# The up projection's high-part products joined to 512 columns, over two sets of banks, with the work beside the projections held to its place

## The chip, the cores and the metric

The kernel runs on one core of one Trainium2 chip. The metric is device microseconds (us) of the whole kernel, one launch; lower is better. Engines: PE is TensorE (matrix products), DVE is VectorE, ACT is ScalarE, POOL is GpSimd, SP is SyncE, which issues the weight loads. PSUM is the memory into which PE accumulates, in banks of 128 x 512 fp32; SBUF is the on-chip working memory.

## The reference

One layer of a diffusion backbone for 256 latent tokens with 256 context tokens, model width 2048, all in float32:

```
qa, ka, va, qb, kb, vb, rb, gf, gb, gate_a, gate_b = proj(modulate(x, g_mix, mod_x[0], mod_x[1]))
qa, ka = apply_rope(qa, cos, sin), apply_rope(ka, cos, sin)
...                                    # the same projection of ctx
o_attn = windowed_attention(qa, ka, va, cka, cva, attn_sink)
o_gla  = latent_gla(qb, kb, vb, gf, gb, sf, sb)
x = x + mod_x[2] * merge_branches(o_attn, o_gla, rb, gate_a, gate_b, gla_norm, w_attn_o, w_gla_o, w_out)
x = x + mod_x[5] * conv_ffn(modulate(x, g_ffn, mod_x[3], mod_x[4]), w_up, conv_w, conv_b, w_down)

def conv_ffn(h, w_up, conv_w, conv_b, w_down):
    u = h @ w_up                                           # 2048 x 11264
    u = sum(up[:, j:j + T] * conv_w[j] for j in range(3)) + conv_b   # centred, along the tokens
    a, g = jnp.split(u, 2, axis=-1)
    return (jax.nn.silu(a) * g) @ w_down                   # 5632 x 2048
```

`mod_x` are six vectors of length 2048, silu(c) @ w_mod + b_mod; part 5 is the gate of the feed-forward's output, so it is wanted only by the down projection.

## The kernel before

**Weights in chunks.** Every large weight matrix is streamed once from HBM in chunks of 256 rows x 512 columns (512 KB). `wload` issues the load on SP into one of seven `raw` buffers. `wsplit` then makes two float32r tiles of it under high priority: `whi` (ACT, L61, a copy that rounds) and `wlo` (DVE, L62, raw minus whi), three buffers each. Activations are kept as a hi and a lo tile in the same way, and a product is hi*hi + lo*hi + hi*lo. There are 568 chunks in the run, 176 of them of `w_up`.

**Two forms of projection.** `proj_nat` holds the activations still and streams the weights: matmuls of 512 columns, lines L176 and L177 (whi with the two parts of the activations) and L181 (wlo). `proj_T` holds the weights still and streams the 256 tokens, so that the result stands transposed (features on the partitions, tokens along the row): matmuls of 256 columns, L203 (activation hi, with whi and then with wlo) and L206 (activation lo with whi). The feed-forward's up projection uses `proj_T`, since the convolution runs along the tokens.

**The up projection.** It has 22 runs of eight chunks: eleven column blocks of 512, each once for the side under silu (side 0) and once for the other (side 1). Six blocks form the first half, five the second, and each half is followed by its part of the down projection. A run accumulates into two banks of the `acc` pool (four banks), two 256-token groups in each. At its end `up_evac` empties them: ACT's Identity with the middle convolution tap and the bias (L923), two multiply-adds on DVE out of PSUM for the other taps (L924, L926), then silu (L929) or the product with side 0 (L931) and the split for the down projection.

**Work beside the projections.** At each chunk `tick()` runs. It lets off work that `defer(n, fn)` put off by n chunks (transposes that need a DVE result), it steps a generator (`beside`: the gated linear attention `gla_A`, or windowed attention), and it steps the background `bg_steps`, which is `mod_latent`: w_mod times silu(c) for one part, on DVE, out of loads that use the same seven `raw` buffers (L264 the first step of a column group, L266 the others). Part 5 runs this way beside the first half of the up projection.

```
def tick():
    for e in later:
        e[0] -= 1
    while later and later[0][0] < 0:
        later.pop(0)[1]()
```

**What sets the order.** The framework's scheduler, not the source order alone, places the instructions of each engine when the kernel is built, by readiness in its own model and by priority. Each engine then runs its list in order: an instruction that waits holds up everything behind it on that engine. Names that matter below: `sr` (the gated attention output, last written at L826) and `m` (the merged branches, L857) are transposed on PE at L816 into `pto`; `ptk` (L711) is the same for the normed keys; `pa` (L534, L599) are scores of the gated attention.

## Time and profile before

| what | value |
|---|---|
| median of three runs | 2056.09 us (2054.43 to 2057.13) |
| profiled execution, its own time | 2061.47 us |
| profiled execution, its span | 2059.7 us |
| mean granted TensorE clock | 0.989 |
| PE busy | 1998.4 us (97%), 11792 matmul records |
| DVE busy | 1399.2 us (68%) |
| ACT busy | 932.7 us (45%) |
| HBM traffic | 411.7 MB, 200 GB/s over the span |

Busy shares are means over stages that differ: a row of "windows" gives one stretch of the span, with the busy time and the count of instructions of each engine, the granted clock as a share of full speed (PEclk) and the share of the DMA engines in use. In the rows of "waits" stand the engine, the tile and line that waited, what it waited for, the total, the count and the longest of them. In the chain of waits a row like "PE acc L203 x9" is a run of nine matmuls one behind another, with the start and the length of the run, so that its length over nine is the spacing of these matmuls. Grouped rows read "busy, mean ns of one | idle before, and what ended it".

### The profile page before, as it was taken

What the parts mean: (1) busy time and instruction counts of PE and PEld (TensorE: products, weight loads), DVE (VectorE), ACT (ScalarE), POOL (GpSimd) and SP (SyncE); (2) the same over time, 40 slices, a digit from 0 to 9 for tenths busy, and PEclk for the clock granted to TensorE, in tenths of its full rate; (3) what the DMA queues carried; (4) which work ended last, traced back from release to release, by engine and by line L of the source; (5) the groups of instructions that cost most, each with busy time, mean ns of one, the idle gap of its engine ahead of it and who ended that gap; (6) DMA issues with size and microseconds to landing.
All of it is one profiled execution on the core that took longest, in us unless ns stands there. A gap on an engine that the chain in (4) does not pass through costs nothing.

```text
span 2059.7 us, 30028 instructions
## 1 busy us (share of the span) xinstructions
PE 1998.4 (97%) x11792; PEld 1727.0 (84%) x11792; DVE 1399.2 (68%) x2149; ACT 932.7 (45%) x1306; POOL 38.9 (2%) x62
## 2 busy tenths in 40 slices
PE   6999999999999999999999999899999999999998
PEld 4778888888787777788788888899999889999987
DVE  4657577887758888777776455877787455556654
ACT  4323464552345665444344444544445334445532
POOL 0001000001000000000000000000000000000000
PEclk8999999999999999999999999899999999999999
DMA  9977322346553466788886766576776666666563
GB/s 346 360 261 217 95 82 83 92 134 203 162 153 113 135 194 198 254 274 273 275 267 218 230 211 205 177 252 226 235 260 208 201 192 191 182 182 183 184 214 112
DMA packets 214350, 413.71 MB, mean 201 GB/s; under 512 B 12548, under 2 KB 21092, under 8 KB 213184
## 3 DMA queue, kind: packets, MB, share of 16 engines
q1 hardware_dynamic: 212320, 406.89, 62.0%
q0 software_dynamic: 1360, 4.74, 0.8%
q8 instruction: 92, 1.51, 0.3%
q14 instruction: 50, 0.41, 0.1%
q10 hardware_dynamic: 528, 0.17, 0.0%
HBM read 409.63 MB, written 2.11 MB: 200 GB/s over the span
## 4 chain that ended last, share of the span: by engine, by line
PE 78%; DVE 9%; DMA 8%; ACT 2%; issue 2%; DVEq 0%; POOL 0%; ACTq 0%; SPq 0%
PE acc L203 20%; PE acc L176 13%; PE acc L177 13%; PE acc L181 13%; PE acc L206 10%; DMA raw<-in_w_mod 8%; DVE wlo L62 3%; DVE macc L266 3%; PE pm L227 1%; PE pa L534 1%; PE po L620 1%; ACT whi L61 1%; PE pa L599 1%; PE ptp L776 1%; PE poa L782 0%
## 5 line engine op out<-in xcount | busy, mean ns | idle before, releaser
L61 ACT ACTIVATE whi<-raw 128x1024 fp32r<-128x1024 f32 x568 | 601.0, 1060 | 833.9 <-PE acc L177 512.4
L62 DVE TENSOR_TENSOR wlo<-raw,whi 128x1024 fp32r<-128x1024 f32 x568 | 693.9, 1226 | 359.6 <-ACT whi L61 327.0
L203 PE MATMUL acc<-h2h,whi 128*128 128x256 f32 x1408 | 347.4, 284 | 1.5 <-ACT h2h L377 1.5
L206 PE MATMUL acc<-h2l,whi 128*128 128x256 f32 x1408 | 346.9, 284 | 0.0
L266 DVE SCALAR_TENSOR_TENSOR macc<-raw,ccol,macc 128x512 f32<-128x512 f32 x240 | 180.3, 751 | 137.3 <-DMA raw<-in_w_mod 133.9
L203 PEld LDWEIGHTS acc<-h2h,whi 128*128 128x128 f32 x1408 | 271.5, 193 | 2.0 <-ACT h2h L377 1.8
L206 PEld LDWEIGHTS acc<-h2l,whi 128*128 128x128 f32 x1408 | 271.4, 193 | 0.2
L203 PE MATMUL acc<-h2h,wlo 128*128 128x256 f32 x1408 | 198.5, 284 | 1.7 <-DVE wlo L62 1.7
L203 PEld LDWEIGHTS acc<-h2h,wlo 128*128 128x128 f32 x1408 | 182.4, 193 | 1.9 <-DVE wlo L62 1.9
L176 PE MATMUL acc<-whi,h00hi 128*128 128x512 f32 x352 | 141.0, 400 | 0.9 <-DVE kb L394 0.6
L176 PE MATMUL acc<-whi,h01hi 128*128 128x512 f32 x352 | 139.8, 397 | 0.0
L177 PE MATMUL acc<-whi,h00lo 128*128 128x512 f32 x352 | 139.7, 397 | 0.0
L177 PE MATMUL acc<-whi,h01lo 128*128 128x512 f32 x352 | 137.8, 391 | 0.0
L176 PE MATMUL acc<-whi,ah 128*128 128x512 f32 x352 | 137.1, 389 | 0.0
L177 PE MATMUL acc<-whi,al 128*128 128x512 f32 x352 | 137.0, 389 | 0.0
L181 PE MATMUL acc<-wlo,h00hi 128*128 128x512 f32 x352 | 98.2, 394 | 0.0
L181 PE MATMUL acc<-wlo,h01hi 128*128 128x512 f32 x352 | 96.9, 393 | 0.5 <-DVE wlo L62 0.5
L181 PE MATMUL acc<-wlo,ah 128*128 128x512 f32 x352 | 94.1, 389 | 0.0
L176 PEld LDWEIGHTS acc<-whi,h00hi 128*128 128x128 f32 x352 | 66.7, 190 | 14.7 <-ACT h00hi L377 0.7
L181 PEld LDWEIGHTS acc<-wlo,h00hi 128*128 128x128 f32 x352 | 66.1, 189 | 13.9 <-DVE wlo L62 0.3
L181 PEld LDWEIGHTS acc<-wlo,ah 128*128 128x128 f32 x352 | 66.1, 188 | 13.8
L176 PEld LDWEIGHTS acc<-whi,ah 128*128 128x128 f32 x352 | 66.1, 188 | 13.7
(369 smaller groups left out, 3267.7 us busy)
## 6 DMA issues: line engine op xcount, KB each, us to landing
raw<-in_w_in SPq DMA_DIRECT2D x208, 512.0 KB, 4.4
raw<-in_w_up SPq DMA_DIRECT2D x176, 512.0 KB, 3.9
raw<-in_w_mod SPq DMA_DIRECT2D x128, 512.0 KB, 4.2
raw<-in_w_down SPq DMA_DIRECT2D x88, 512.0 KB, 4.3
mraw<-in_w_mod SPq DMA_DIRECT2D x32, 1024.0 KB, 12.0
raw<-in_w_attn_o SPq DMA_DIRECT2D x32, 512.0 KB, 4.7
raw<-in_w_gla_o SPq DMA_DIRECT2D x32, 512.0 KB, 5.1
raw<-in_w_out SPq DMA_DIRECT2D x32, 512.0 KB, 4.1
```

Of the source, the lines that this page charges most:

```text
L61: S.activation(hi, src, AF.Copy)
L62: V.tensor_tensor(lo, src, hi.bitcast(F32), op=ALU.subtract)
L176: PE.matmul(banks[i], ahi, hi[:, k, :], start=(kt == kts[0]), stop=False)
L177: PE.matmul(banks[i], alo, hi[:, k, :], start=False, stop=False)
L181: PE.matmul(banks[i], l(kt)[0], lo[:, k, :], start=False, stop=(kt == kts[-1]))
L203: PE.matmul(o, w_, ahi, start=(kt == kts[0] and b == 0 and part == 0), stop=(kt == kts[-1] and part == 1), skip_group_check=True)
L206: PE.matmul(o, w_, alo, start=False, stop=False, skip_group_check=True)
L227: PE.matmul(a[0][q:q + 32, :], cS[:, kt, :], raw[:, k, :], start=(kt < 4), stop=(kt >= 12))
L266: V.scalar_tensor_tensor(a[0], raw[:, k, :], ccol[:, kt:kt + 1], a[0], op0=ALU.mult, op1=ALU.add)
L534: PE.matmul(pa[:, t, :], k2[:, dt, t * P:(t + 1) * P], q2[:, dt, tq * P:(tq + 1) * P], start=(dt == 0), stop=(dt == 1))
L599: PE.matmul(pa[:, t, :], kk[:, dt, t * P:(t + 1) * P], qq[:, dt, :], start=(i == 0 and dt == 0), stop=(i == 1 and dt == 1))
L620: PE.matmul(po, x_, y_[:, s, :], start=(n == 0), stop=(n == 11))
```

## The change

It has two parts. **The up projection** goes through a new function, `proj_pair`. The hi and the lo part of the activations now lie side by side in one tile, `h2` (before: tiles `h2h` and `h2l`), so that one matmul of 512 columns multiplies a hi weight block with both; the two results fall into the two halves of a bank. The lo weight block is multiplied with the hi activations alone, 256 columns, into the first half. A run now takes four banks: side 0 the four `acc` banks, side 1 the bank and the three side banks that the work beside the projections uses elsewhere (`accs`). `up_evac` first adds the halves of each bank: ACT copies the second half into `us` (L973), DVE adds the first (L974), and the convolution then reads `us` in SBUF (ACT L975, DVE L976 and L978).

**The work beside** keeps its place among the products: `mm_b` and `turn_b` tie a matmul or a transpose to come, in PE's list, behind the last product that was issued before the tick. `tick()` lets off every due entry, not only those at the head of the list. The deferrals grow: `rb_evac` and `mg_evac` from 1+t to 3+t chunks, `ka_evac` from 1+i//2 to 2+i; the column sums of w_mod's part 5 are let off in `up_banks` at the start of a side 0 run; `gla_A` yields once more ahead of the `pa` products of L599, at 1.65 instead of 1.5 steps a chunk.

```diff
--- before.py
+++ after.py
@@ -61,6 +61,25 @@
+    last, pin = [None], [None]
+
+    def mm(*a, **k):
+        last[0] = PE.matmul(*a, **k).ins
+
+    def after(i):
+        if pin[0] is not None:
+            tc.add_manual_dep(i.ins, pin[0].name, mybir.DependencyInfo(
+                mybir.DependencyClass.NoSync, mybir.DependencyReason.DATA), reason="place among the products")
+        return i
+
+    def mm_b(*a, **k):
+        return after(PE.matmul(*a, **k))
+
+    def turn_b(*a):
+        return after(PE.transpose(*a))
+
@@ -132,10 +151,13 @@
     def tick():
 
+        pin[0] = last[0]
         for e in later:
             e[0] -= 1
-        while later and later[0][0] < 0:
-            later.pop(0)[1]()
+        due = [e for e in later if e[0] < 0]
+        later[:] = [e for e in later if e[0] >= 0]
+        for e in due:
+            e[1]()
...
+        pin[0] = None
@@ -200,12 +223,30 @@
+    def proj_pair(w, c0, kts, pair, banks, evac):
+
+
+        for k0 in kts[::2]:
+            tick()
+            nk = min(2, kts[-1] + 1 - k0)
+            hi, lo = wsplit(w[k0 * P:(k0 + nk) * P, c0:c0 + 512])
+            for f in range(4):
+                for k in range(nk):
+                    mm(banks[f], hi[:, k, f * P:(f + 1) * P], pair(k0 + k),
+                              start=(k0 + k == kts[0]), stop=False, skip_group_check=True)
+            for f in range(4):
+                for k in range(nk):
+                    mm(banks[f][:, 0:T], lo[:, k, f * P:(f + 1) * P], pair(k0 + k)[:, 0, :],
+                              start=False, stop=(k0 + k == kts[-1]), skip_group_check=True)
+        for f in range(4):
+            evac(f, banks[f])
@@ -592,11 +633,12 @@
         yield
+        yield
         pa = bank("pa", (P, 2, T), side=True)
@@ -638,7 +680,7 @@
-        beside[:] = [gla_A(h, kb, qbt, res), 1.5, 0.0]
+        beside[:] = [gla_A(h, kb, qbt, res), 1.65, 0.0]
@@ -703,15 +745,15 @@
-        defer(1 + i // 2, turn)
+        defer(2 + i, turn)
@@ -824,7 +866,7 @@
-            defer(1 + t, lambda: to_T(s_, gh, gl, j, t))
+            defer(3 + t, lambda: to_T(s_, gh, gl, j, t))
@@ -855,7 +897,7 @@
-            defer(1 + t, lambda: to_T(a2[t], mh, ml, j, t))
+            defer(3 + t, lambda: to_T(a2[t], mh, ml, j, t))
@@ -897,15 +939,22 @@
-    h2h = [M(f"h2h{i}", [P, 8, T], F32R) for i in range(2)]
-    h2l = [M(f"h2l{i}", [P, 8, T], F32R) for i in range(2)]
+    h2 = [M(f"h2{i}", [P, 4, 2, T], F32R) for i in range(4)]
...
-    bg_steps.extend(mod_latent([(5, gcol2)]))
+    sums = []
+    bg_steps.extend(mod_latent([(5, gcol2)], sums.append))
     bg_rate[:] = [0.36, 0.0]
-    h2 = [lambda kt: (h2h[kt // 8][:, kt % 8, :], h2l[kt // 8][:, kt % 8, :])]
+
+    def up_banks(side):
+
+        if side == 0:
+            while sums:
+                defer(3, sums.pop(0))
+            return [acc.tile([P, 512], F32, name="acc", tag="acc") for _ in range(4)]
+        return [bank("accs", side=(f > 0)) for f in range(4)]
@@ -915,16 +964,21 @@
-            def up_evac(p_, b, side, j=j, u=u, i=i, ah=ah, al=al):
+            def up_evac(f, b, side, j=j, u=u, i=i, ah=ah, al=al):
+                p_ = f // 2
                 uu = u[side][p_]
-                for f in range(2):
-                    fi = side * 44 + j * 4 + 2 * p_ + f
-                    d, bf = uu[:, f, :], b[:, f * T:(f + 1) * T]
-                    S.activation(d, bf, AF.Identity, scale=cw1[:, fi:fi + 1], bias=cb[:, fi:fi + 1])
-                    V.scalar_tensor_tensor(d[:, 1:T], bf[:, 0:T - 1], cw0[:, fi:fi + 1], d[:, 1:T],
-                                           op0=ALU.mult, op1=ALU.add)
-                    V.scalar_tensor_tensor(d[:, 0:T - 1], bf[:, 1:T], cw2[:, fi:fi + 1], d[:, 0:T - 1],
-                                           op0=ALU.mult, op1=ALU.add)
+                d = uu[:, f % 2, :]
+                fi = side * 44 + j * 4 + f
+                us = W2("fa", "us", [P, T])
+                S.activation(us, b[:, T:2 * T], AF.Copy)
+                V.tensor_tensor(us, b[:, 0:T], us, op=ALU.add)
+                S.activation(d, us, AF.Identity, scale=cw1[:, fi:fi + 1], bias=cb[:, fi:fi + 1])
+                V.scalar_tensor_tensor(d[:, 1:T], us[:, 0:T - 1], cw0[:, fi:fi + 1], d[:, 1:T],
+                                       op0=ALU.mult, op1=ALU.add)
+                V.scalar_tensor_tensor(d[:, 0:T - 1], us[:, 1:T], cw2[:, fi:fi + 1], d[:, 0:T - 1],
+                                       op0=ALU.mult, op1=ALU.add)
+                if f % 2 == 0:
+                    return
...
-            proj_T(w_up, j * 512, ALL, h2, lambda p_, b: up_evac(p_, b, 0))
-            proj_T(w_up, DFF + j * 512, ALL, h2, lambda p_, b: up_evac(p_, b, 1))
+            for side in range(2):
+                proj_pair(w_up, side * DFF + j * 512, ALL, lambda kt: h2[kt // 4][:, kt % 4, :, :],
+                          up_banks(side), lambda f, b, side=side: up_evac(f, b, side))
```

What the change does to the engines' lists shows best in three places. In the rows the numbers behind the names tell buffers apart.

The first is PE within one chunk of the up projection; `acc` is the bank, `whi` and `wlo` the chunk's two parts, held still, and `h2h`, `h2l` and `h22` the activations that stream. Before, the first pair of products of each bank and the last rows (each pair stands four times in a row):

```order
L203 MATMUL acc_13999<-h2h0_10918,whi_14039 128x256
L206 MATMUL acc_13999<-h2l0_10920,whi_14039 128x256
...
L203 MATMUL acc_14000<-h2h0_10918,whi_14039 128x256
L206 MATMUL acc_14000<-h2l0_10920,whi_14039 128x256
...
L203 MATMUL acc_13999<-h2h0_10918,wlo_14040 128x256 x4
L203 MATMUL acc_14000<-h2h0_10918,wlo_14040 128x256 x4
```

The same chunk now, whole:

```order
L68 MATMUL acc_11872<-h22_10920,whi_11981 128x512 x2
L68 MATMUL acc_11873<-h22_10920,whi_11981 128x512 x2
L68 MATMUL acc_11874<-h22_10920,whi_11981 128x512 x2
L68 MATMUL acc_11875<-h22_10920,whi_11981 128x512 x2
L68 MATMUL acc_11872<-h22_10920,wlo_11982 128x256 x2
L68 MATMUL acc_11873<-h22_10920,wlo_11982 128x256 x2
L68 MATMUL acc_11874<-h22_10920,wlo_11982 128x256 x2
L68 MATMUL acc_11875<-h22_10920,wlo_11982 128x256 x2
```

Sixteen matmuls of 256 columns with whi (L203 and L206 by turns) have become eight of 512, recorded at L68 since `mm` issues them; the eight of 256 columns with wlo are as many as before, in four banks instead of two.

The second is PE at the end of the last `rb` block, where the two token tiles of `sr` are transposed into `pto` among the first chunks of the next projection, `w_attn_o`. Rows within a chunk are left out at "...".

```order
L181 MATMUL acc_7656<-wlo_7664,oh0_5422 128x512 x2
L816 MATMUL pto_7679<-ident_86,sr_7641 128x128 x4
L176 MATMUL acc_7655<-whi_7688,oh0_5422 128x512
...
L181 MATMUL acc_7656<-wlo_7689,oh0_5422 128x512 x2
L816 MATMUL pto_7704<-ident_86,sr_7645 128x128 x4
L176 MATMUL acc_7655<-whi_7717,oh0_5422 128x512
```

And now:

```order
L68 MATMUL acc_7656<-wlo_7664,oh0_5422 128x512 x2
L68 MATMUL acc_7655<-whi_7681,oh0_5422 128x512
...
L68 MATMUL acc_7656<-wlo_7682,oh0_5422 128x512 x2
L68 MATMUL acc_7655<-whi_7703,oh0_5422 128x512
...
L68 MATMUL acc_7656<-wlo_7704,oh0_5422 128x512 x2
L81 MATMUL pto_7719<-ident_86,sr_7641 128x128 x4
L68 MATMUL acc_7655<-whi_7728,oh0_5422 128x512
...
L68 MATMUL acc_7656<-wlo_7729,oh0_5422 128x512 x2
L81 MATMUL pto_7744<-ident_86,sr_7645 128x128 x4
```

The first transpose has moved from behind that projection's first chunk to behind its third, and the second from behind the second chunk to behind the fourth.

The third is DVE in the first half of the up projection, around one background load: the row whose `raw` buffer this load takes over, and the row that uses the load.

```order
L62 TENSOR_TENSOR wlo_12640<-raw_12637,whi_12639 128x1024
L62 TENSOR_TENSOR wlo_12674<-raw_12671,whi_12673 128x1024
L266 SCALAR_TENSOR_TENSOR macc_12573<-raw_12855,ccol_96,macc_12573 128x512
L280 COPY gcol2_115<-pcl_12630 32x4
L62 TENSOR_TENSOR wlo_12704<-raw_12701,whi_12703 128x1024
```

Now, around the load in the same place of SP's list:

```order
L62 TENSOR_TENSOR wlo_12361<-raw_12358,whi_12360 128x1024
L62 TENSOR_TENSOR wlo_12383<-raw_12380,whi_12382 128x1024
L974 TENSOR_TENSOR us_12294<-accs_12097,us_12294 128x256
...
L62 TENSOR_TENSOR wlo_12438<-raw_12435,whi_12437 128x1024
L976 SCALAR_TENSOR_TENSOR u_11871<-us_12315,cw0_1989,u_11871 128x255
L62 TENSOR_TENSOR wlo_12460<-raw_12457,whi_12459 128x1024
...
L62 TENSOR_TENSOR al_10974<-u_11871,ah_10971 128x512
L321 COPY gcol2_115<-pcl_12402 32x4 x2
L307 SCALAR_TENSOR_TENSOR macc_12269<-raw_12501,ccol_96,macc_12269 128x512
L62 TENSOR_TENSOR wlo_12508<-raw_12505,whi_12507 128x1024
```

Before, the load `raw_12855` takes the buffer that the row above its use lets go; now the corresponding load `raw_12501` takes the buffer that L62 of `wlo_12361` lets go, and 24 rows stand between that row and its use, of which some are shown.

More of the change, by code (lines that the diff above doesn't have):

```diff
@@ L175, in proj_nat @@
                     ahi, alo = l(kt)
-                    PE.matmul(banks[i], ahi, hi[:, k, :], start=(kt == kts[0]), stop=False)
-                    PE.matmul(banks[i], alo, hi[:, k, :], start=False, stop=False)
+                    mm(banks[i], ahi, hi[:, k, :], start=(kt == kts[0]), stop=False)
+                    mm(banks[i], alo, hi[:, k, :], start=False, stop=False)
             for i, l in enumerate(lhs):
@@ L180, in proj_nat @@
                     kt = k0 + k
-                    PE.matmul(banks[i], l(kt)[0], lo[:, k, :], start=False, stop=(kt == kts[-1]))
+                    mm(banks[i], l(kt)[0], lo[:, k, :], start=False, stop=(kt == kts[-1]))
         for i in range(len(lhs)):
@@ L202, in proj_T @@
                             ahi, alo = r(kt)
-                            PE.matmul(o, w_, ahi, start=(kt == kts[0] and b == 0 and part == 0),
+                            mm(o, w_, ahi, start=(kt == kts[0] and b == 0 and part == 0),
                                       stop=(kt == kts[-1] and part == 1), skip_group_check=True)
                             if part == 0:
-                                PE.matmul(o, w_, alo, start=False, stop=False, skip_group_check=True)
+                                mm(o, w_, alo, start=False, stop=False, skip_group_check=True)
         for i in range(len(banks)):
             evac(i, banks[i])
+    def proj_pair(w, c0, kts, pair, banks, evac):
[13 more added lines that the diff above has]
+            evac(f, banks[f])
     ALL = list(range(KT))
@@ L240, in mod_both, with mod_latent @@
         return [lambda k0=k0: step(k0) for k0 in range(0, KT, nk)]
-    def mod_latent(parts):
+    def mod_latent(parts, put=lambda fn: defer(3, fn)):
         seq = [(part, dst, j, k0) for part, dst in parts for j in range(4) for k0 in range(0, KT, 2)]
@@ L282, in out @@
                     V.tensor_tensor(d, d, bmod[:, b0:b0 + 4], op=ALU.add)
-                defer(3, out)
+                put(out)
         return [lambda i=i: step(i) for i in range(len(seq))]
@@ L290, in rows_from_cols @@
         pt = bank("pt_" + name, (KT, P), side=True)
-        PE.transpose(pt, col, ident)
+        turn_b(pt, col, ident)
         row = sm.tile([KT, P], F32, name="row", tag="t128", bufs=2)
@@ L680, in layer_kernel, with norm_rope @@
                                 norms[:, i, 64 - u * 64:128 - u * 64], op=ALU.mult)
-    def norm_rope(b, r, t):
-        y = W2("fc", "y", [P, 4, P])
+    def norm_rope(b, r, t, tag):
+        y = W2(tag, "y", [P, 4, P])
         S.activation(y, b.rearrange("p (h d) -> p h d", h=4), AF.Copy)
@@ L705, in ka_evac @@
     def ka_evac(i, b):
-        z = norm_rope(b, rk if i < 2 else None, i % 2)
+        z = norm_rope(b, rk if i < 2 else None, i % 2, "fa")
         def turn():
@@ L710, in turn @@
             for h in range(4):
-                PE.transpose(pt[:, h, :], z[:, h, :], ident)
+                turn_b(pt[:, h, :], z[:, h, :], ident)
             split(kTh[:, :, i * P:(i + 1) * P], kTl[:, :, i * P:(i + 1) * P], pt)
-        defer(1 + i // 2, turn)
+        defer(2 + i, turn)
     bg_rate[0] = 1.6
@@ L725, in evac @@
         def evac(t, b):
-            z = norm_rope(b, rq, t)
+            z = norm_rope(b, rq, t, "fc")
             def turn():
@@ L730, in turn @@
                 for h in range(4):
-                    PE.transpose(pt[:, h, :], z[:, h, :], ident)
+                    turn_b(pt[:, h, :], z[:, h, :], ident)
                 split(qT[:, 0, :, t * P:(t + 1) * P], qT[:, 1, :, t * P:(t + 1) * P], pt)
@@ L750, in attend @@
                 pS = bank("pS", side=True)
-                PE.matmul(pS, qh, kTh[:, g, :], start=True, stop=False)
-                PE.matmul(pS, qh, kTl[:, g, :], start=False, stop=False)
-                PE.matmul(pS, ql, kTh[:, g, :], start=False, stop=True)
+                mm_b(pS, qh, kTh[:, g, :], start=True, stop=False)
+                mm_b(pS, qh, kTl[:, g, :], start=False, stop=False)
+                mm_b(pS, ql, kTh[:, g, :], start=False, stop=True)
                 s_ = W2("fa", "s", [P, 512])
@@ L775, in attend @@
                 for h in range(4):
-                    PE.transpose(pt[:, h, :], sc[h][:, k * P:(k + 1) * P], ident)
+                    turn_b(pt[:, h, :], sc[h][:, k * P:(k + 1) * P], ident)
                 th = W2("fb", "pth", [P, 512], F32R)
@@ L781, in attend @@
                 vk_h, vk_l = vah[:, k, g * P:(g + 1) * P], val[:, k, g * P:(g + 1) * P]
-                PE.matmul(po, vk_h, th, start=(k == 0), stop=False)
-                PE.matmul(po, vk_h, tl, start=False, stop=False)
-                PE.matmul(po, vk_l, th, start=False, stop=(k == 3))
+                mm_b(po, vk_h, th, start=(k == 0), stop=False)
+                mm_b(po, vk_h, tl, start=False, stop=False)
+                mm_b(po, vk_l, th, start=False, stop=(k == 3))
                 if k in (1, 3):
@@ L815, in to_T @@
         for k in range(4):
-            PE.transpose(pt[:, k, :], src[:, k * P:(k + 1) * P], ident)
+            turn_b(pt[:, k, :], src[:, k * P:(k + 1) * P], ident)
         q4 = slice((j % 2) * 4, (j % 2) * 4 + 4)
@@ L884, in turn @@
                 for k in range(4):
-                    PE.transpose(pt[:, k, :], x1[t][:, j * 512 + k * P:j * 512 + (k + 1) * P], ident)
+                    turn_b(pt[:, k, :], x1[t][:, j * 512 + k * P:j * 512 + (k + 1) * P], ident)
                 dst = x1T[j // 2][:, (j % 2) * 4:(j % 2) * 4 + 4, t * P:(t + 1) * P]
@@ L899, in layer_kernel @@
     rrow = token_rows("fb", "rrow", r1)
[L900 to L901 removed]
+    h2 = [M(f"h2{i}", [P, 4, 2, T], F32R) for i in range(4)]
     for kt in range(KT):
         xk = x1T[kt // 8][:, kt % 8, :]
[L904 removed]
+        affine_split(h2[kt // 4][:, kt % 4, 0, :], h2[kt // 4][:, kt % 4, 1, :], xk, rrow,
                      scale2[:, kt:kt + 1], shift2[:, kt:kt + 1])
[L906 removed]
+    sums = []
+    bg_steps.extend(mod_latent([(5, gcol2)], sums.append))
     bg_rate[:] = [0.36, 0.0]
[L908 removed]
+    def up_banks(side):
[4 more added lines that the diff above has]
+        return [bank("accs", side=(f > 0)) for f in range(4)]
     w_up, w_down = A["w_up"][0], A["w_down"][0]
@@ L933, in up_evac @@
                     split(ah[i // 2][:, q, :], al[i // 2][:, q, :], uu)
-            proj_T(w_up, j * 512, ALL, h2, lambda p_, b: up_evac(p_, b, 0))
-            proj_T(w_up, DFF + j * 512, ALL, h2, lambda p_, b: up_evac(p_, b, 1))
+            for side in range(2):
+                proj_pair(w_up, side * DFF + j * 512, ALL, lambda kt: h2[kt // 4][:, kt % 4, :, :],
+                          up_banks(side), lambda f, b, side=side: up_evac(f, b, side))
         if half == 0:
             assert not bg_steps
+            while sums:
+                sums.pop(0)()
             flush()
```

13 lines of the change are left out of this document (6 added, 7 removed).

## The prediction

> **What bounds the kernel now.** The page's first part comes first, then the waits of PE, and then single stretches.
>
> ```profile
> span 2059.7 us, 30028 instructions
> PE 1998.4 (97%) x11792; PEld 1727.0 (84%) x11792; DVE 1399.2 (68%) x2149; ACT 932.7 (45%) x1306; POOL 38.9 (2%) x62
> ```
>
> PE is busy for 97% of the span, so there are two ways to gain: make the stream of products shorter, or take away its waits and the slow clock that follows them. The waits, by PE's list, for the tiles that the change touches:
>
> ```profile
> PE ptk L711 <- DVE sq L700: 5.0, 1, 5.0
> PE pa L599 <- DVE kf L592: 4.9, 4, 2.1
> ...
> PE pto L816 <- DVE sr L826: 3.9, 1, 3.9
> PE pa L534 <- DVE q L554: 3.4, 4, 1.5
> PE pto L816 <- DVE m L857: 3.2, 2, 2.3
> ...
> PE acc L203 <- DVE wlo L62: 1.7, 1, 1.7
> ```
>
> Those are single events, 22 us in all. Two stretches of the up projection, the first half and a piece of the second:
>
> ```profile
> 1305.00:1572.00 267.00, 265.26 (x2199) 264.57 (x2199) 206.15 (x299) 134.43 (x170) 0.00 (x0) 1.00 0.73 233
> 1760.00:1940.00 180.00, 180.00 (x1502) 180.00 (x1501) 110.91 (x143) 89.62 (x111) 0.00 (x0) 1.00 0.62 183
> ```
>
> PE never stops in the second, at full clock: 180.00 over 1502 matmuls is 0.1198 us each, so here the spacing of matmuls of 256 columns is all that counts. In the first half PE is the bound too (265.3 of 267), but DVE with 206.2 is not far off once its own waits are added:
>
> ```profile
> DVE macc L266 <- DMA raw<-in_w_mod: 40.4, 15, 4.5
> ...
> DVE macc L264 <- DMA raw<-in_w_mod: 3.5, 2, 2.9
> ```
>
> The 40.4 and 3.5, 43.9 us, are DVE standing before a background load of w_mod, with the next `wlo` queued behind; PE paid 1.7 for it at most, so this list has hardly any slack left unseen.
>
> **The up projection's products.** The chain of waits gives the spacing by runs of equal matmuls:
>
> ```profile
> 487.78 1.81 PE acc L181 x8
> 1309.15 1.08 PE acc L203 x9
> ```
>
> 1.81/8 = 0.2263 us for 512 columns, 1.08/9 = 0.120 for 256. Two matmuls of 256 cost 0.240, one of 512 costs 0.2263: the same columns, one fixed cost less. A chunk was 24 x 0.120 = 2.88; it becomes 8 x 0.2263 + 8 x 0.120 = 2.77, so 0.110 less. Over 176 chunks that is **-19.3 us**: 96 chunks (10.5) in the first half, 80 (8.8) in the second. The 0.2263 stems from products that stream weights past held activations; in the change weights are held and activations stream. Bounds: 2 x 0.120 for 512 columns would give nothing; an end below has no row (the second window's 0.1198 leaves 0.2263 where it is). I keep 0.2263, since 512 columns in one bank are the same there.
>
> The Trainium skill ("TensorE: Matmul & The Clock Gate", section "Back-to-back issue gap") puts the isolated spacing at N/2.4 + 2.5 ns, thus only 2.5 ns of fixed cost: an estimate by it is 8 x 2.5 ns x 176 = 3.6 us instead of 19.3. The rows disagree: 0.120 and 0.2263 leave 13.7 ns between two of 256 and one of 512.
>
> **What the joining adds.** Each of the 22 runs of eight chunks now empties four banks: four ACT copies and four DVE adds more, and eight multiply-adds that read SBUF rather than PSUM. Their nearest rows, of the whole run, and then rows of DVE in the first-half window:
>
> ```profile
> L565 DVE TENSOR_TENSOR segs<-segs 128x256 f32<-128x256 f32 x32 | 13.4, 420 | 1.2 <-ACT q L552 1.2
> L394 DVE TENSOR_TENSOR qb<-qb,acc 128x512 f32<-128x512 f32 x16 | 10.4, 684 | 19.1 <-PE acc L203 19.1
> L376 DVE SCALAR_TENSOR_TENSOR x1T<-x1T,scale,rrow 128x256 f32<-128x256 f32 x16 | 6.9, 481 | 1.6 <-ACT rrow L329 1.6
> L923 ACT ACTIVATE u<-acc,cb,cw 128x256 f32<-128x256 f32 x88 | 44.4, 554 | 23.1 <-DVE u L926 23.1
> ```
>
> ```profile
> L924 DVE SCALAR_TENSOR_TENSOR u<-acc,cw,u 128x255 f32<-128x255 f32 x44 | 19.2, 476 | 0.0
> ...
> L62 DVE TENSOR_TENSOR al<-u,ah 128x512 fp32r<-128x512 f32 x10 | 6.5, 688 | 0.0
> L931 DVE TENSOR_TENSOR u<-u 128x512 f32<-128x512 f32 x10 | 6.4, 686 | 0.0
> ```
>
> The multiply-add costs the same from SBUF (481) as from PSUM (476). The add lies between 0.42 (same size, SBUF) and 0.684 (twice the size, one operand in PSUM); I take 0.42. A copy on ACT is at most 0.554. In the first-half window 44 adds are 18.5 us for DVE and 44 copies up to 24 for ACT. ACT goes from 134 to 158 of some 257, and stays hidden. For DVE the budget is needed: the window holds 267/2.88 = 92.7 chunks, which PE would now do in 256.8 us. DVE was busy 206.2 and waited 43.9 for w_mod; with the adds it needs 206.2 + 18.5 + 43.9 = 268.6, more than PE has, unless the waits shrink.
>
> They should. A w_mod load takes the `raw` buffer that a split seven loads earlier gives back, and needs 4.2 us to land:
>
> ```profile
> raw<-in_w_mod SPq DMA_DIRECT2D x128, 512.0 KB, 4.2
> ...
> 1470.15 1.54 DVE L266 SCALAR_TENSOR_TENSOR macc<-raw,ccol,macc 128x512 f32<-128x512 f32 x2 [4.52 <-DMA raw<-in_w_mod]
> ```
>
> Where release and use are neighbours in DVE's list, DVE waits the whole landing; where other work stands between, only the rest of it. Adding up, by the list before and the durations above, what DVE's work between release and use leaves of 4.2 us, over the 32 loads, gives 40.9 us, beside 43.9 measured; the list of the change gives 27.5 in the same way, since evacuation rows now stand between. DVE then needs 206.2 + 18.5 + 27.5 = 252.2 of 256.8. That is nearly full, so some late `wlo` will reach PE: between nothing and, with the waits unchanged, 268.6 - 256.8 = 11.8. I take **+2 us**, near the low end, as 252.2 is below the bound but the waits come in lumps of up to 4.5 against PE's lead of at most three `wlo` buffers, 8.3 us. In the second half no background runs (DVE 110.9 of 180) and the adds are hidden. Side 1's four banks are those of the work beside; there only w_mod's sums use one, and they are put into side 0's runs. A set comes back after eight chunks, 22 us, which side 1's evacuation, 4 x 0.42 + 8 x 0.48 + 2 x (0.686 + 0.688) = 8.3 us of DVE work, does not exceed.
>
> **The later transposes.** At the end of the `rb` block and at the first merge block PE stood before its transposes:
>
> ```profile
> 859.82 0.74 PE L816 MATMUL pto<-ident,sr 128*128 128x128 f32 x4 [3.89 <-DVE sr L826]
> ...
> 1023.56 0.66 PE L816 MATMUL pto<-ident,m 128*128 128x128 f32 x4 [0.87 <-DVE m L857]
> ...
> 1026.56 0.66 PE L816 MATMUL pto<-ident,m 128*128 128x128 f32 x4 [2.34 <-DVE m L857]
> ```
>
> DVE's list keeps `sr`'s last step behind the third chunk's `wlo`. PE now reaches the transpose behind that chunk's lo products, which need the `wlo` ahead, so the 3.9 vanishes. At the merge block the second transpose comes one chunk (2.72 us, 12 x 0.2263) later, enough for 2.3; the first keeps its 0.87. Together **-6.2 us**. What was queued behind each was all of the next chunk's products; what is late next is the split into `gl` and `ml`, wanted many chunks on. Both stalls also cost clock:
>
> ```profile
> 860.00:865.00 5.00, 5.00 (x21) 4.07 (x19) 3.76 (x7) 1.66 (x2) 0.00 (x0) 0.66 0.76 231
> 865.00:870.00 5.00, 5.00 (x25) 4.15 (x23) 4.40 (x5) 1.82 (x3) 0.00 (x0) 1.00 0.83 216
> 1027.00:1032.00 5.00, 5.00 (x17) 3.94 (x16) 4.19 (x11) 1.66 (x2) 0.00 (x0) 0.66 0.83 263
> ```
>
> 0.66 for 5 us after each, then 1.00: 2 x 5 x 0.34 = **-3.4 us**.
>
> **The other moves: nothing.** For `ptk` PE now does a chunk's products first and comes 2.7 us later, but in DVE's list one more split (1.2 us) and the second token tile's steps have come in front of the awaited step, about 2.5 us; the 5.0 stays, within 0 and 7.6 with its clock (next fence). For `pa` the extra yield and the rate move PE's place and DVE's by about as much, 2.5 against 2.4 us a time: within 2 us of zero. If either cover were gone, the waits of 4.9 and 3.4 above are the whole stake.
>
> ```profile
> 541.00:548.00 7.00, 6.15 (x20) 5.07 (x21) 5.65 (x10) 3.69 (x5) 0.00 (x0) 0.63 0.00 0
> ```
>
> 0.63 over 7 us is 2.6 us of lost clock behind the 5.0.
>
> **Sum.** -19.3 + 2 - 6.2 - 3.4 = -26.9. The profiled execution's own time is 2061.5, which makes 2034.6; it lies 5.4 above the median 2056.1 of the runs, so the forecast on their scale is **2029 us**.
>
> **The rivals.**
>
> *VectorE becomes the bound in the first half.* The waits for w_mod stay at 43.9 instead of 27.5, because the release that a load waits for comes later by as much as its use. Then the half ends by DVE, 11.8 late instead of 2: 2029 + 9.8 = 2039. For it: 206 busy plus 44 waiting in 267. Against: the list has more rows between release and use.
>
> *The joining saves little.* With held weights the joined products take nearly as long as two of 256, say 0.2375, near the upper bound of 0.240: the term is 8 x 0.0025 x 176 = 3.5 instead of 19.3, so 2029 + 15.8 = 2045. For it: no row has 512 columns streaming past held weights in this kernel. Against it: the fixed cost read from 0.120 and 0.2263 is 13.7 ns (2 x 0.120 - 0.2263), in two streams that differ in the same way. The Trainium skill's section named above would have it at 2.5 ns, and so this result.
>
> *`wlo` late at the end of every run: slower.* If the evacuation's 8.3 us of DVE work stand in one lump ahead of the splits, they use up PE's whole lead of 8.3, and each wait for w_mod that falls there goes to PE in full: 2.7 (40.4/15) at each of the first half's 12 run ends, 32 us, so 2061. It decides from a lump of 8.3 us onward. Against it: the list has a split between every few evacuation rows.
>
> *The waits for `ptk` and `pa` go as well.* If PE comes late enough, 5.0 + 2.6 fall away: 2021, and 2017 with the four `pa` waits of L599 (4.9) nearly gone. For it: each is placed later on PE. Against: DVE's steps moved too.
>
> **How the numbers follow.** Forecast 0.62; VectorE bound 0.20; `ptk` and `pa` gone 0.10; little saved by joining 0.04; slower 0.04. The range is 2017 to 2044: from the fourth rival's end up past VectorE's case, with 5 us for the lumps on top of it; it leaves out the slower case, the case of 2045, and tails of the others, about 0.15. Runs of this kernel spread over 0.13%, so 0.2% (4 us) is about what can be told from no change. All cases but the slower one lie below 2052; its 0.04, with 0.03 for mixtures that end near it, makes faster 0.93, same 0.03, slower 0.04.
>
> **What would show it.** In the chain of waits of the changed kernel, runs of eight matmuls in 1.81 and 0.96 us in the up projection, 2.77 a chunk. `pto` on `sr` gone from PE's waits, `pto` on `m` at about 0.9, and no clock of 0.66 after them; `ptk` still near 5. DVE's waits for w_mod in the first half at 25 to 30 us, and PE's on `wlo` there at 2 to 4; at 40 and 12 VectorE is the bound. I'd be wrong altogether if `wlo` waits of PE recurred at the run ends, or if 512 columns took 0.240.

## The result, and the profile after

The changed kernel takes 2039.95 us (median of four runs, 2036.63 to 2042.93) against 2056.61 us before (2054.43 to 2057.76): 16.7 us less, a ratio of 0.9923 with a 95% interval of 0.991 to 0.9936. Timed once more, in one session with the first variants below, it took 2039.67 us against 2058.53, a ratio of 0.9906 (0.989 to 0.9922). The forecast was 2029 (2017 to 2044): the direction and the range hold, the gain is some 10 us smaller than forecast.

The head of the page of the changed kernel:

```profile
span 2036.9 us, 27383 instructions
PE 1978.8 (97%) x10384; PEld 1644.1 (81%) x10384; DVE 1429.5 (70%) x2237; ACT 961.1 (47%) x1394; POOL 42.5 (2%) x62
```

PE's waits, for the tiles of the prediction and those that are new:

```profile
PE acc L68 <- DVE wlo L62: 4.2, 8, 1.4
...
PE po L78 <- DVE v3l L62: 2.3, 1, 2.3
PE ptk L81 <- DVE sq L742: 2.3, 1, 2.3
...
PE ptx L81 <- issue: 1.7, 1, 1.7
```

Both `pto` waits are gone, the first one at `m` too, of which the forecast kept 0.9 us. In their place stand eight waits for `wlo`, 4.2 us in all, a wait for `v3l` at the end of the gated attention, and one before w_out's first transposes that the profile puts down to "issue". None of the eight lies in the up projection, whose first half the next two rows show, followed by a piece of the second half (columns as in the windows before):

```profile
1297.00:1566.00 269.00, 269.00 (x1531) 236.09 (x1532) 229.58 (x354) 152.73 (x220) 0.00 (x0) 0.99 0.73 238
1746.00:1926.00 180.00, 180.00 (x1030) 158.31 (x1029) 124.82 (x181) 102.41 (x146) 0.00 (x0) 1.00 0.59 188
```

PE is busy without a gap in both. VectorE's waits for w_mod in that first half:

```profile
DVE macc L307 <- DMA raw<-in_w_mod: 17.1, 10, 2.9
```

With one of 2.0 at L305 they are 19.1 us, where they were 43.9 before. The new and changed DVE instructions of the evacuation, grouped:

```profile
L978 DVE SCALAR_TENSOR_TENSOR u<-us,cw,u 128x255 f32<-128x255 f32 x44 | 21.0, 479 | 0.0
...
L974 DVE TENSOR_TENSOR us<-acc,us 128x256 f32<-128x256 f32 x24 | 9.0, 417 | 0.0
```

The add takes 0.417 us (0.42 taken), the multiply-add out of SBUF 0.479 (0.481), and the copy on ACT (L973) 0.381 (at most 0.554).

**Where the time went.** The 568 weight splits stand in the same sequence in all these kernels, so the start of the n-th on ACT is a milestone common to every trace. The table gives the time between milestones, in us, in three profiled executions whose work beside stands as before (the two of the kernel before, and the variant with the joined up projection alone, described below) and in two of the change:

| chunks | stage | before | before, second profile | up part alone | change | change, second profile |
|---|---|---|---|---|---|---|
| 64 to 82 | end of gated attention, keys | 120.5 | 117.1 | 120.5 | 119.3 | 121.3 |
| 152 to 160 | end of rb | 28.4 | 24.7 | 25.2 | 22.7 | 22.7 |
| 160 to 208 | first merge block | 135.0 | 136.3 | 135.3 | 136.4 | 138.2 |
| 208 to 216 | its transposes | 28.7 | 30.5 | 29.4 | 24.8 | 23.9 |
| 216 to 248 | second merge block | 88.8 | 88.8 | 88.8 | 91.2 | 91.1 |
| 280 to 288 | first evacuation of w_out | 22.7 | 22.7 | 22.7 | 24.6 | 24.7 |
| 311 to 408 | most of up's first half, start of its down projection | 282.0 | 281.8 | 272.5 | 272.5 | 272.5 |
| 448 to 528 | up, second half | 230.0 | 230.0 | 223.3 | 223.3 | 223.3 |

The up projection gains 9.4 and 6.7 us in the last two rows. These rows don't hold it whole: the first half is chunks 304 to 400, and a split runs ahead of the product that uses it, so some chunks of the down projection stand in them. PE's own products give the whole. In the second half their starts, from the first to the last, span 223.35 us in both profiles of the change and 230.27 in both of the kernel before: 6.9 less. From the split of chunk 288 to the start of the first half's last product it takes 334.7 and 334.6 us, against 345.4 and 345.5: 10.8 less, so 17.7 together.

The later transposes gain 2.0 to 5.7 us at rb and 3.9 to 6.6 at the merge's own transposes. Then some 1.8 us come back in the first merge block (by the means), 2.4 in the second and 1.9 at w_out.

### The profile page after: what moved, and what is told of

It reads as the page before. It is cut to its first block, busy times and chain, and to the rows that moved or that the text cites. A ratio compares the mean times of both kernels' runs of the same rounds, so it can differ in the third digit from the quotient of the medians.

```text
span 2036.9 us, 27383 instructions
## 1 busy us (share of the span) xinstructions
PE 1978.8 (97%) x10384; PEld 1644.1 (81%) x10384; DVE 1429.5 (70%) x2237; ACT 961.1 (47%) x1394; POOL 42.5 (2%) x62
## 4 chain that ended last, share of the span: by engine, by line
PE 56%; DMA 8%; DVE 5%; issue 1%; ACT 0%; DVEq 0%; ACTq 0%
PE acc L68 40%; PE accs L68 12%; DMA raw<-in_w_mod 8%; DVE macc L307 2%; DVE wlo L62 1%; PE poa L78 1%; PE pS L78 1%; PE ptp L81 1%; PE pto L81 0%; ACT whi L61 0%; PE ptq L81 0%; DMA raw<-in_w_gla_o 0%; PE ptx L81 0%; DVE macc L305 0%; DVE s L811 0%
## 5 line engine op out<-in xcount | busy, mean ns | idle before, releaser
L62 DVE TENSOR_TENSOR wlo<-raw,whi 128x1024 fp32r<-128x1024 f32 x568 | 693.0, 1224 | 324.5 <-ACT whi L61 303.4
L68 PE MATMUL acc<-h,whi 128*128 128x512 f32 x704 | 178.3, 395 | 2.2 <-DVE h L419 2.2
L68 PE MATMUL accs<-h,whi 128*128 128x512 f32 x704 | 176.3, 392 | 0.0
L68 PEld LDWEIGHTS acc<-h,whi 128*128 128x128 f32 x704 | 127.6, 190 | 25.6 <-DVE h L419 2.5
L68 PEld LDWEIGHTS accs<-h,whi 128*128 128x128 f32 x704 | 126.6, 189 | 22.6
L68 PE MATMUL acc<-whi,h00hi 128*128 128x512 f32 x352 | 140.5, 399 | 1.6 <-DVE kb L435 0.6
L68 PE MATMUL acc<-whi,h01hi 128*128 128x512 f32 x352 | 139.9, 398 | 0.0
L68 PE MATMUL acc<-whi,h00lo 128*128 128x512 f32 x352 | 138.3, 393 | 0.0
L68 PE MATMUL acc<-whi,h01lo 128*128 128x512 f32 x352 | 138.0, 392 | 0.0
L68 PE MATMUL acc<-whi,al 128*128 128x512 f32 x352 | 137.1, 389 | 0.0
L68 PE MATMUL acc<-whi,ah 128*128 128x512 f32 x352 | 137.0, 389 | 0.0
L68 PEld LDWEIGHTS acc<-h,wlo 128*128 128x128 f32 x704 | 96.2, 190 | 7.0
L68 PEld LDWEIGHTS accs<-h,wlo 128*128 128x128 f32 x704 | 96.0, 190 | 6.9
L68 PE MATMUL acc<-wlo,h01hi 128*128 128x512 f32 x352 | 97.1, 394 | 1.7 <-DVE wlo L62 1.7
L68 PE MATMUL acc<-h,wlo 128*128 128x256 f32 x704 | 98.3, 282 | 0.0
L68 PE MATMUL accs<-h,wlo 128*128 128x256 f32 x704 | 98.2, 282 | 0.0
L68 PE MATMUL acc<-wlo,h00hi 128*128 128x512 f32 x352 | 97.8, 393 | 0.0
L68 PE MATMUL acc<-wlo,ah 128*128 128x512 f32 x352 | 94.4, 389 | 0.0
L68 PEld LDWEIGHTS acc<-whi,h00hi 128*128 128x128 f32 x352 | 66.4, 189 | 15.7 <-DVE val L62 1.0
L68 PEld LDWEIGHTS acc<-wlo,h01hi 128*128 128x128 f32 x352 | 65.5, 188 | 15.8 <-DVE wlo L62 2.5
```

Of the source, the lines that this page charges most:

```text
L62: V.tensor_tensor(lo, src, hi.bitcast(F32), op=ALU.subtract)
L68: last[0] = PE.matmul(*a, **k).ins
```

## The experiments

**The change once more, unaltered.**

> The changed kernel once more, unaltered, for a second profile and for its time on the same chip as the three variants. If the 22.8 us between the two profiled executions are the change's worth, the ratio is 0.989 (2034 us); if the 16.7 us between the medians are, it is 0.992 (2040 us). In the trace: joined products of 512 columns at 0.230 us on average in the up projection (1.84 a chunk instead of 1.81), small waits of PE for wlo between the rb block and the end of the merge, 4 to 6 us in all. The wait before w_out's first transposes (1.7 us in the first profile, with the gate's broadcast landing late) is gone if it was chance.

2039.67 us, 0.9906 (0.989 to 0.9922), between the two values expected. Its profile is the last column of the table; waits of PE for `wlo` between rb and merge 4.7 us, and the "issue" wait came again (1.8), so it isn't chance.

**The kernel before once more, unaltered.**

> The kernel before once more, for a second profile. In the first one PE waited 3.9 us for sr's transpose, with 5 us of slow clock behind; with the same list around it, the variant with the joined up projection alone waited 2.2 us and its clock stayed at full speed. If the first profile had an unusually long wait there, this one has about 2.2 us and no slow clock, and its time lies near 2057; if the 3.9 is typical, it comes again and the time is near 2061.

The profiled execution took 2057.57 us instead of 2061.47, and its waits for the transposes were:

```profile
PE pto L816 <- DVE m L857: 3.3, 2, 2.3
...
PE ptk L711 <- DVE sq L700: 2.1, 1, 2.1
PE pto L816 <- DVE sr L826: 1.7, 1, 1.7
```

The wait for `sr` is 1.7, not 3.9, that for `ptk` 2.1, not 5.0, from the same list. And the clock behind the wait for `sr` stayed up, while behind that for `m` it fell again:

```profile
855.00:865.00 10.00, 10.00 (x47) 8.26 (x46) 8.59 (x11) 4.11 (x5) 0.00 (x0) 1.00 0.83 255
...
1021.00:1026.00 5.00, 4.74 (x13) 3.89 (x14) 4.55 (x11) 0.78 (x2) 0.00 (x0) 0.50 0.77 238
```

So the first profile caught the wait for `sr` unusually long: 3.7 of its us between chunks 152 and 160 were not the kernel's usual time. The wait for `ptk` varies too, but 5.0 isn't out of the way: the variant described next has 4.5 from the same work beside.

**The up projection alone.** The kernel before with `proj_pair`, the two sets of banks and the new evacuation; deferrals and places as before:

```diff
-            proj_T(w_up, j * 512, ALL, h2, lambda p_, b: up_evac(p_, b, 0))
-            proj_T(w_up, DFF + j * 512, ALL, h2, lambda p_, b: up_evac(p_, b, 1))
+            for side in range(2):
+                proj_pair(w_up, side * DFF + j * 512, ALL, ..., up_banks(side), ...)
```

> The kernel before with the joined up projection alone (two sets of banks, and the column sums of part 5 let off in side 0 runs, which the banks require); the work beside keeps its places and deferrals. My account of the traces: 0.086 us a chunk x 176 = 15.1 us less, and about 1 us less of stalls in the first half, so -14 to -17 us, near 2041. The prediction's term (0.110 a chunk, +2 for VectorE): -17.3, 2039. If VectorE were the bound in the first half: -8 or less there, 2047 or more. Waits before the pto transposes (3.9 and 3.2 us) stay.

2041.03 us, 17.5 below the kernel before in the same session (2058.53): 0.9912 (0.9896 to 0.9929). In its profile both rows of the up projection are those of the change. The up part is nearly the whole gain.

**The work beside alone.** The change with the old up projection:

```diff
-                proj_pair(w_up, side * DFF + j * 512, ALL, ..., up_banks(side), ...)
+            proj_T(w_up, j * 512, ALL, h2, lambda p_, b: up_evac(p_, b, 0))
+            proj_T(w_up, DFF + j * 512, ALL, h2, lambda p_, b: up_evac(p_, b, 1))
```

> The changed kernel with the old up projection (256-column products, two banks, the old evacuation); all of the work beside as in the change. My account: the pto waits go (-9.6 with their slow clock), but 4 us come back as waits for wlo in the merge, where VectorE's busy time and its waits for w_mod fill the window; with 2 less at ptk that is -4 to -7 us, near 2051. The prediction: -9.6, 2047. Rival: nothing measurable, within 2 us of before, if PE is held to VectorE's pace all the way to the merge's end.

2056.62 us, 1.9 below before: 0.9992 (0.9981 to 1.0003), not to be told from nothing. -17.5 and -1.9 add to -19.4, beside -18.9 for the whole change in that session. My expectation of -4 to -7 missed too; the rival held.

**The early transposes back.**

```diff
-            defer(3 + t, lambda: to_T(s_, gh, gl, j, t))
+            defer(1 + t, lambda: to_T(s_, gh, gl, j, t))
...
-            defer(3 + t, lambda: to_T(a2[t], mh, ml, j, t))
+            defer(1 + t, lambda: to_T(a2[t], mh, ml, j, t))
```

> The changed kernel with the transposes of rb and merge let off after 1+t chunks again, everything else as in the change. The list then has rb's transposes where they stood before, and the first merge block's pair two chunks and one chunk ahead of where they stood before. The prediction's view (each wait costs its length and the clock after it): +5.6 for rb, and at the merge block up to 5.4 + 2.3 and 1.7 of clock, so +10 to +15, 2050 to 2055. My account (VectorE is the pace of this stage, so PE's waits there are partly paid anyway): +3 to +8, 2043 to 2048. Rival: below +2, if waits for wlo make up all of it.

2042.81 us, 3.1 more than the change in the same session (intervals of the two ratios overlap: 0.9905 to 0.9937, 0.989 to 0.9922). PE's waits from the rb block to the end of the merge in this variant:

```profile
PE pto L81 <- DVE m L899: 5.0, 2, 3.9
PE pto L81 <- DVE sr L868: 1.8, 1, 1.8
PE acc L68 <- DVE wlo L62: 1.0, 2, 0.5
```

and in the second profile of the change:

```profile
PE acc L68 <- DVE wlo L62: 4.7, 9, 0.9
```

The 6.8 us of waits for transposes were taken away, and 3.7 more of waits for `wlo` came. What VectorE does meanwhile, in that same profile of the change, first its window and then its waits there:

```profile
887.00:1002.00 115.00, 112.45 (x493) 90.14 (x492) 83.97 (x110) 47.68 (x50) 0.00 (x0) 1.00 0.82 272
```

```profile
DVE macc L307 <- DMA raw<-in_w_mod: 29.0, 17, 3.1
DVE macc L305 <- DMA raw<-in_w_mod: 2.5, 3, 1.0
```

Busy 84.0 and waiting 31.5 fill the 115, the first part of the merge. A PE that comes sooner there finds no `wlo` ahead.

**The gate's row earlier.**

```diff
-    defer(4, lambda: gate1.append(rows_from_cols("gate1", gcol1)))
+    defer(1, lambda: gate1.append(rows_from_cols("gate1", gcol1)))
```

> The changed kernel with the gate of the attention branch turned into a row three chunks earlier (deferred by 1 instead of 4). With the later transposes the last transposes of the merge stand right before the gate's, ACT copies them first, and the gate's small write is issued 0.05 us after a weight load (in the kernel before 0.76 us ahead of one); it takes 3.8 us instead of 2.0 and PE waits 1.6 to 1.8 us for the broadcast in all three profiles with the later transposes, and in none without. If so that wait goes: -1.7 us, 2038. Rival: the gate's load then collides elsewhere and delays a weight chunk: no change.

The wait behind the "issue" row is one for the gate's broadcast. The landing times of the small write ahead of it, in the kernel before and then in the change, columns size and us to landing:

```profile
dgate<-row POOLq DMA_DIRECT2D x1, 8.0 KB, 2.0
```

```profile
dgate<-row POOLq DMA_DIRECT2D x1, 8.0 KB, 3.8
```

With the earlier row the small write, now issued 1.1 us ahead of the next weight load, lands in 1.9 us, PE's wait is gone and chunks 280 to 288 take 22.7 again. The whole takes 2039.84 us, no change: its profile has 139.9 us in the first merge block, against 136.4 to 138.2, which is as much as the gate gave or more. PE's waits for `wlo` are 8.2 us there, where the change's two profiles have 4.2 and 4.7. The mechanism is shown, its worth on the whole is not.

**The gated attention's steps back.**

```diff
-        yield
         yield
...
-        beside[:] = [gla_A(h, kb, qbt, res), 1.65, 0.0]
+        beside[:] = [gla_A(h, kb, qbt, res), 1.5, 0.0]
```

> The changed kernel with gla_A's steps as before (one yield ahead of the pa products of L599, 1.5 steps a chunk). In the stretch of chunks 64 to 73, the end of the gated attention, five profiles with the change take 65.0 us and three without it 61.1, with a wait of PE of 2.3 us for v3's lo part. If the extra yield and the rate cause this, the stretch takes 61 again, and the next (chunks 73 to 82, where PE waits for ptk) stays at 56: -4 us, 2036. If ptk's wait grows by what is gained, as in the first profile of the kernel before (59.3 instead of 56.0): no change, 2040.

Chunks 64 to 73 take 61.1 us, so the extra yield and the rate do cost 3.9 there: in the change 2.3 us of PE's wait for `v3l`, and behind it 3.3 us at a granted clock of 0.50, which lose 1.7. 73 to 82 take 57.0, with `ptk`'s wait at 3.4. The whole: 2039.95 us, no change. Chunks 280 to 288 took 26.8 in that profile, behind a longer wait for the gate (2.4).

**The order of the joined products.** Two of 512 and two of 256 columns by turns:

```diff
             for f in range(4):
                 for k in range(nk):
                     mm(banks[f], hi[:, k, f * P:(f + 1) * P], pair(k0 + k), ...)
-            for f in range(4):
                 for k in range(nk):
                     mm(banks[f][:, 0:T], lo[:, k, f * P:(f + 1) * P], pair(k0 + k)[:, 0, :], ...)
```

> The changed kernel with the joined products and the 256-column ones of a chunk by turns: for each block of 128 features two of 512 columns, then two of 256, instead of eight and eight. In the changed kernel the first five joined products after a run of 256-column ones take 0.233, 0.236, 0.228, 0.232 and 0.231 us instead of 0.227, 0.02 more a chunk. If each switch from 256 to 512 columns costs that, a chunk with four switches takes 2.85 us: +10 us over the change, near 2050. If the run of eight short products is what leaves something behind that five long ones must make up, two short ones leave a quarter of it or nothing: a chunk takes 2.77 to 2.80, 2036 to 2040.

The eighty chunks of the second half take 223.5 us, 223.3 in the change: 2.79 a chunk in either order. A cost of 0.02 per switch is refuted, and the order doesn't win the 0.02 back. The whole took 2044.15 us, 0.9932 (0.9915 to 0.9948); in its profile chunks 360 to 408 lost 2.1 us, with three waits of PE for `wlo`, 1.8 in all, where the change has none: each chunk's `wlo` is wanted sooner. The rest of the 4.5 us to the change's 2039.67 isn't traced.

**512 columns throughout.** This kernel computes one term more, lo times lo, in the up projection:

```diff
-                    mm(banks[f][:, 0:T], lo[:, k, f * P:(f + 1) * P], pair(k0 + k)[:, 0, :], ...)
+                    mm(banks[f], lo[:, k, f * P:(f + 1) * P], pair(k0 + k), ...)
```

> The changed kernel with 512 columns in all sixteen products of a chunk of the up projection: the wlo products take hi and lo of the activations too, which adds the lo*lo term that the kernel otherwise leaves out. It costs time; what counts is the spacing in an unmixed stream with held weights. If 0.227 us, the 0.2305 of the change comes from standing among products of 256 columns; if 0.2305 or more, it belongs to this form of product (held weights, activations that stream). A chunk of 16 x 0.227 takes 3.63 us, of 16 x 0.2305 3.69; against 2.79 the whole kernel is 148 or 158 us longer, 2188 or 2198.

2186.2 us. The chains of waits in the second half, of the change and then of this variant:

```profile
1799.88 11.17 PE acc L68 x64
```

```profile
1805.44 24.71 PE accs L68 x109
```

In the change 64 matmuls, four chunks, take 11.17 us, 2.79 a chunk; here 109 of 512 columns take 24.71, 0.2267 each, the spacing forecast. So held weights are not the reason. Among products of 256 columns the joined ones take 0.230 on average; why is open.

**Own buffers for w_mod.**

```diff
-    wr = pool(name="wr", bufs=7)
+    wr = pool(name="wr", bufs=5)
...
-                raws[i] = wload(w_mod[k0 * P:k0 * P + 256, c0:c0 + 512])
+                raws[i] = wload(w_mod[k0 * P:k0 * P + 256, c0:c0 + 512], "rawm", 2)
```

The two buffers have the tag `rawm`, and a background load is also tied, in the list, behind the last product ahead of its tick, since nothing else keeps it from coming early.

> The changed kernel with the seven raw buffers divided: five for the weights, two of their own for the background loads of w_mod, with those loads held to their place. If VectorE standing before w_mod's loads (49 us between the rb block and the end of the merge, and some 40 in the first half of the up projection) is what makes PE wait for wlo there, those waits of VectorE fall to under 10 us, PE's waits for wlo (4.2 and 4.7 us in the two profiles) go, and the time is 3 to 6 us less, 2034 to 2037. Rival: five buffers are too few for the weights, whi comes late instead, and the kernel is slower, 2042 or more. If VectorE's waits are not the cause, no change.

2028.73 us, 0.9854 (0.9837 to 0.9871): 11 below the change, more than expected. In this profile PE has no wait between the rb block and the merge's end, and 160 to 248 takes 245.4 us where six profiles with shared buffers take 252.4 to 255.7 (before, its repeat and the up part alone 252.4, 255.7, 253.5; the change, its repeat and the early transposes 252.5, 253.1, 254.7). But VectorE's waits for w_mod there did not fall:

```profile
DVE macc L310 <- DMA raw<-in_w_mod: 51.5, 38, 2.9
```

In the first half of the up projection they fell to 3.6. And 6 to 8 us of the gain lie elsewhere, in chunks 64 to 82 (113.6 instead of 119.3 to 121.3): the waits for `v3l` and `ptk` are gone, and with them the slow clock behind.

The next two variants, which have own buffers too, tell which of this recurs. Chunks 64 to 82 take 113.2 and 113.0 us there (64 to 73 alone 60.8, with the extra yield kept), and VectorE's waits for w_mod in them are 5.2 to 7.0 us in all three profiles against 17.7 and 18.8 in the two of the change. But 160 to 248 takes 251.2 and 251.9, hardly less than with shared buffers: the 245.4 did not come again. Whether the separate buffers or the place of the loads in the list does it isn't shown, as each of these runs has both.

**Own buffers, early transposes.** Both edits above together.

> The changed kernel with own buffers for w_mod and the transposes of rb and merge let off after 1+t chunks again. With shared buffers these early transposes cost 3.1 us on the medians, since waits for wlo had taken most of the gain of the later ones. If VectorE's shortage there was the reason, the later transposes are worth their whole wait once the buffers are apart: +8 to +12 us over own buffers alone, 2037 to 2041. If not, +3 again, 2032.

2029.85 us, 1.1 above own buffers alone, within the spread. I had expected 8 to 12, so the theory that the later transposes would pay in full with buffers apart falls. In its profile PE waits 4.6 us for `m` and 0.9 for `sr`, and not at all for `wlo` between rb and merge.

**Own buffers, earlier gate.**

> The changed kernel with five raw buffers for the weights and two of their own for w_mod, and the gate's row three chunks earlier as well. With own buffers PE still waited 2.0 us before w_out's first transposes, with 2.8 us of slow clock behind it, and those eight chunks took 26.5 us instead of 22.7; the earlier gate alone brought that stretch to 22.7 in the changed kernel. If the two add: 3.8 us less than with own buffers alone, near 2025. If the gate's wait is only moved, 2029.

2028.96 us, 0.9859 (0.9844 to 0.9874), the same as own buffers alone. Chunks 280 to 288 fell from 26.5 to 22.7, and 160 to 208 took 137.1 instead of 132.6. There PE waits for `wlo` again, though the buffers are apart:

```profile
PE acc L68 <- DVE wlo L62: 4.5, 7, 1.5
```

That is as much as the 4.6 for `m` with the early transposes. So own buffers did not end VectorE's shortage in the merge: with the later transposes one profile has no such wait, the other has these. The best times are thus 2028.7 to 2029.0, 1.4 to 1.5% below before.

## Why the prediction was right or wrong

**The joined products: right, mis-sized.** The term was -19.3, from 0.2263 us for 512 columns. The second half, where nothing else moves, gives (230.27 - 223.35)/80 = 0.0865 us a chunk, 15.2 over 176. The 0.2263 holds in an unmixed stream (0.2267 with weights held), not among products of 256 columns (0.230). The estimate with 2.5 ns of fixed cost comes to 8 x 2.5 ns x 176 = 3.5 us, as the second rival has it, not 3.6; the measured 15.2 is far from it.

**VectorE in the first half: right in kind, wrong in sign.** I took +2 from waits for w_mod of 27.5; they were 19.1, and PE never waited for `wlo` there. 10.8 - 96 x 0.0865 = 2.5 us were won instead, waits for `wlo` of 1.7 and 1.1 us in the two profiles before among them. The durations behind the budget were right to 0.003 us for both VectorE instructions. With the term before, -17.3 forecast stands beside -17.7 in the traces and -17.5 on the medians. That is luck: two errors of some 4 us each cancelled.

**The later transposes: the step that failed.** "Together -6.2 us" and "2 x 5 x 0.34 = -3.4 us" took each wait at its length in one execution, and as paid in full. Two things are shown. The length at rb was an unusually long one: 1.7 us in the repeat and 2.2 in the variant with the same work beside, with no slow clock. And the sentence that "what is late next is the split into `gl` and `ml`" was wrong: what was late next was `wlo`. In the first half of the up projection I added VectorE's waits to its busy time; at the merge I did not, and there the two fill the window of its first 115 us. Taking the transposes back costs 3.1 us on the medians, not 9.6, and all the work beside together makes 1.9, not to be told from nothing. So 6.5 to 7.7 of the some 10 us that are missing stand in this step; the two sessions alone, 16.7 and 18.9, differ by 2.2, and the rest is open. The clock's fall behind `m` is real and recurs, and its removal shows in chunks 208 to 216.

**The other moves.** "Nothing" for `ptk` and `pa` held in the sum (chunks 64 to 82 take 119.3 and 121.3 us, beside 117.1 to 120.5 without the change), not in the parts: 3.9 us lost at the end of the gated attention, as much or less won at the keys. The wait for `ptk` is 2.1 and 5.0 us in two profiles of one kernel. The gate's broadcast, 1.9 us, I had not seen: later transposes stand right before the gate's, ACT copies them first, and its small write meets a weight load.

**The conversion.** I took 5.4 us off since the profiled execution was that much above the median. But one of the waits whose removal I counted, that for `sr`, was part of what made it long, 3.7 us beside the second profile, which lay at 2057.57. A sum against the first execution may count that wait at its length; a forecast from the median may not.

**The rivals.** 2039 for VectorE as the bound is close to the result by coincidence, for its mechanism did not act in its place: the first half of the up projection has no such loss, the merge has one. Those of 2045, 2061 and 2021 did not happen. What paces the merge in the end is not settled: with own buffers VectorE still waits 51.5 us for w_mod there, moving the transposes makes 1 us, and executions of nearly the same list differ by 6 us in chunks 160 to 248 (245.4, 251.2 and 251.9).

## What to carry to other kernels

A wait is worth its length only if the next thing behind it has slack: add up busy time and waits of the engine that feeds PE in that very window before counting a removed wait as won. Read a single wait from two profiles of the same kernel before it becomes a term, above all where slow clock may follow it; and read a gain by stages from two profiles as well. Prefetched loads that share a rotation of buffers with the stream they run beside tie the two together. Here separate buffers, with the loads held to their place, were worth 11 us, while moving five kinds of work about gave 2 us, not to be told from nothing.

## What the runs showed of the hardware

- The spacing of matmuls depends on the company: 0.2267 us for 512 columns among their like and 0.120 for 256 among theirs. In runs of eight and eight they take 0.230 and 0.119 on average, in runs of two and two 0.233 and 0.115; a chunk of sixteen takes 2.79 us either way, 0.01 to 0.02 more than the unmixed spacings add up to. Two of 256 at 0.120 less one of 512 at 0.2267 leave 13 ns, the fixed part of a matmul here if all else goes by columns. The Trainium skill ("TensorE: Matmul & The Clock Gate", section "Back-to-back issue gap") has 2.5 ns for the isolated gap; the traces disagree, and decide.
- The length of a wait alone does not tell whether the clock falls. Behind single waits of PE of 1.7 and 1.8 us (`sr`, w_out) it stayed at 1.00. Of waits of 2.0 to 2.3 us, those for the gate with own buffers (2.0), for `ptk` in the second profile before (2.1) and for `v3l` in the change (2.3) were followed by 0.50 for 3.3 to 3.4 us; those for `sr` in the up part alone (2.2) and for `ptk` in the first profile of the change (2.3) were not. The same pair of waits for `m`, 0.9 to 1.0 and 2.3 us, brought 0.50 for 3.4 us in one profile of the kernel before and for 6.7 in the other.
- An 8 KB write issued 0.05 us after a 512 KB load landed in 3.7 to 3.9 us in all seven profiles that have that order; issued 0.8 or 1.1 us ahead of one it landed in 1.8 to 2.0 in the other seven.
